# One decoder layer with two kinds of attention: the first stage in another order, the squares from a token-major copy of the input, both rotary tables on VectorE

## The chip, the cores and the metric

The kernel runs on one core of a Trainium2 chip. Its metric is the device time of one execution in microseconds (us). A core has a matrix engine, TensorE (PE in the profile, its weight loads PEld); VectorE (DVE); ScalarE (ACT), which also evaluates functions such as sine and tanh; GpSimd (POOL); and SyncE (SP), which here issues the loads and stores. Each engine has a queue of its own and works through it in order; semaphores hold an instruction until what it reads is there.

## The reference

The reference is one layer for 512 tokens of width 1024 in float32: retention in 8 heads and a sparse attention in 16 query heads and 2 groups side by side, a gated merge, an MLP, and an input of its own for each layer. What matters here is the beginning:

```
def rms_norm(x, g):
    y = x * lax.rsqrt(jnp.mean(x * x, axis=-1, keepdims=True) + 1e-6)
    return y * g

cos_r, sin_r = rope_tables(positions, 128)     # rotary tables of the retention
cos_n, sin_n = rope_tables(positions, 64)      # and of the sparse attention
h = rms_norm(x, norm_mix_g)
proj = h @ w_in                                # queries, keys, values, gates of both
...                                            # sparse attention: kc, vc are compressed to blocks,
                                               # two more keys and two more values are used as they are
x = x + (p @ w_ple_proj) * sigmoid(rms_norm(x, norm_ple_g) @ w_ple_gate)
```

The product `p @ w_ple_proj` needs nothing of the rest, so it can be formed at any time; here it is formed first and parked in memory.

## The kernel before

**Products.** All large products are float32 products made of three products of rounded float32r parts: `mm3` multiplies high by high, high by low and low by high. Each operand has therefore a high part (`hi`, a rounding copy on ScalarE, L206) and a low part (`lo`, the rest, a subtraction on VectorE, L209). Weights come in `Piece`s, mostly 128 x 1024, in three buffers taken in turn (`raw`); a piece is loaded when the third piece ahead of it is used up, and split in halves of 512 columns. `dense` forms 128 x 512 outputs over the eight k-tiles of the normed input, in two items of twelve products, one for each weight half.

**Order.** The program is a list of `Item`s. `run` emits for each item the weight splits that it still needs, its TensorE work, then `look` weight splits ahead (the high parts on ScalarE, the low parts one step behind on VectorE), and last the item's `post`, the work of the other engines on what it left. The order of emission is the order of each engine's queue.

**The first stage** (`start` to `post_nv`). SP loads the per-layer input, its weights, the input transposed (`xT`, 128 x 8 x 512, four loads of 512 KB), the constants, the gains and the positions. TensorE forms the per-layer input product in two halves of four token tiles (`ps_d`, `ps_v`, `ps_s`; copied to `pp_sb` and stored). Beside it ScalarE squares the tiles of `xT` and VectorE adds them into `acc`; sixteen products with a column of ones (L343) sum them over the partitions, `rsqrt` makes the factor of each token, and `over_partitions` spreads the factors over all partitions (`rb`). `make_h` forms the normed tile `ht` from `xT`, gain and `rb` (L511), its high part on ScalarE (L512) and its low part (L514). Eight items with 304 columns (values of the two exact branches and the branch gates, `w_nv`) multiply the normed tiles, tile by tile as they are made; `post_nv` splits the values into `vcat` (L541, L543) and takes the gates' tanh (L542).

**After that** four dense products follow: compressed values (`vc`, `ps_t`), compressed key (`kc`, `ps_t`), two exact keys (`ps_d`, `ps_v`), and then the two compressions and head 0 of the retention. `post_vc` copies the values twice (`dup`, L600, L601) and adds positions (`blk`, L590); `post_kc` turns the key with the table of the sparse attention (`rope_nsa`: VectorE, then a sum `nr` on GpSimd, L532) and copies it twice (L608, L609).

**Rotary tables.** The angles of 512 tokens lie folded as 128 x 256. `reduced` subtracts multiples of two pi, `folded` does so in three steps of falling size (L386), `ends` takes an absolute value and eight sines on ScalarE (L400, L401), which need ScalarE's sine table (ACT_TABLE_LOAD). The table of the sparse attention (`n`) is reduced on GpSimd in the first stage, with its sines between the halves of `vc`; the table of the retention (`r`) is made on VectorE in head 0, its items put in at three places there:

```
items += [vc[0], table_n[1], vc[1], Item(0, lambda: close("nw", "a0"))]
items += [x for x, at in zip(table_r, (0, 4, 5)) if n == at]
```

Of the kernel before, what the change touches and what calls it, by code (L numbers as in the profile page):

```python
# [16 lines left out]
P = 128  # L17
S = 512
# [14 lines left out]
# columns of the constants  # L33
# [3 lines left out]
# columns of the gains  # L37
# [34 lines left out]
def weave(a, b):  # L72
    """Two lists of items merged in proportion to their costs."""
# [13 lines left out]
class Op:  # L87
    """A step of one engine, for arrange(): its time, the steps it needs, the buffers it takes and gives back."""
# [52 lines left out]
def _layer_kernel(ctx, tc, a, out):  # L141
# [4 lines left out]
    # ------------------------------------------------------------------ pools  # L146
# [17 lines left out]
    # the banks of PSUM: two pairs "s", two singles "t", and the singles "v" and "d"  # L164
# [7 lines left out]
    # ------------------------------------------------------- weights, in pieces  # L172
# [15 lines left out]
    def split(n, low=True, eng=dve):  # L188
        """The two parts of the n-th part of a weight, the low one only with low."""
# [23 lines left out]
    def used(p):  # L213
        """The buffer of p has all its readers: the third piece after it may follow."""
# [4 lines left out]
    def defer(fn):  # L219
        """fn is emitted behind the next item on the tensor engine."""  # L220
        deferred.append(fn)

    def run(items):
# [6 lines left out]
        for it in items:  # L230
# [11 lines left out]
            # the low part one step behind the high part, so that neither engine waits for the other  # L242
# [11 lines left out]
    def mm3(ps, sh, sl, mh, ml, first, last):  # L254
        """ps (+)= (sh + sl).T @ (mh + ml), without the product of the two low parts."""
# [4 lines left out]
    def dense(tag, pieces, xs, post, nsub=2, off=0):  # L260
        """ps[n, tok] = sum over the k-tiles of xs(), as nsub items; post(ps) takes it up."""
# [24 lines left out]
    def rsqrt(v, n, tag, eng=dve):  # L286
        """1 / sqrt(v) of a small [128, n] tile: bit estimate, a step of third and one of second order."""
# [24 lines left out]
    def parts(pool_, t, tag, name, late=False, **kw):  # L312
        """hi and lo float32r parts of the SBUF tile t; the low part behind the next item with late."""
# [10 lines left out]
    # -------------------------------------------------------------- constants  # L324
# [11 lines left out]
    def token_rstd(accs, tag):  # L336
        """Items that leave rstd of each token, [128, 4], in T[tag]."""
# [15 lines left out]
    def over_partitions(tag, dst):  # L353
        """An item that puts T[tag] of each token on every partition of dst()."""
# [11 lines left out]
    def table(pool_, name, ci, cs, tmp):  # L366
# [4 lines left out]
        def reduced(pool=dve):  # L371
            ang, kk, kh, t = T[name] = tmp()
            pool.tensor_copy(kk, T["pos_i"])
# [1251 lines left out]
```

## Time and profile before

| | us |
|---|---|
| timed runs, median of 3 (lowest, highest) | 1291.59 (1290.68, 1291.60) |
| profiled execution, span | 1288.7 |
| TensorE busy in it | 1261.2 |
| VectorE busy | 770.6 |
| ScalarE busy | 530.1 |
| GpSimd busy | 230.4 |

The page of the profile gives the profiled execution as its span, from its first to its last instruction; the timed runs also hold what lies around the span, and are 2.0 to 2.9 us longer than it. A row of the timeline is an instruction (or several alike, x2 and more): its start and duration in us, its engine and line, what it writes and reads by the program's names, and in brackets how long the engine had been idle before it and what ended that. A wait is idle time of an engine put down to the instruction that released it. The granted clock of TensorE is a share of 2.4 GHz.

### The profile page before, as it was taken

The page shows a single profiled execution, that of the slowest core. Times are in us where ns is not written, and L with a number is a line of the kernel's source. Part 1 is how long each engine was busy: PE and PEld are TensorE (multiplying, and loading weights), DVE is VectorE, ACT ScalarE, POOL GpSimd, SP SyncE. Part 2 cuts the span into 40 slices and gives each one's busy share as a digit, 9 for nine tenths or more (in the row PEclk, how much of TensorE's full clock was granted, in tenths as well). Part 3 has the DMA queues.
Part 4 walks back from the last instruction along what each step waited for, and adds up shares of the span by engine and source line. Part 5 has one row for each costly group of instructions (what it writes and reads, how often), then busy time and mean ns, then how long its engine had stood idle before and what let it go on. Part 6 is the DMA issues. An engine that isn't in the chain of part 4 may idle for free.

```text
span 1288.7 us, 16807 instructions
## 1 busy us (share of the span) xinstructions
PE 1261.2 (98%) x6312; PEld 1038.0 (81%) x6312; DVE 770.6 (60%) x1398; ACT 530.1 (41%) x1091; POOL 230.4 (18%) x310
## 2 busy tenths in 40 slices
PE   7999999999999999999999999999999999999996
PEld 6867998988988887787888778888888888888885
DVE  7665664557467477678878864556653235544456
ACT  5644333333233233567877652343322223333333
POOL 5230000000000013357664600000000000000035
PEclk9999999999999999999999999999999999999998
DMA  6532223223223232211111022342232343332221
GB/s 244 176 121 88 75 91 98 74 91 98 75 82 105 68 90 82 66 50 33 34 34 34 17 77 90 120 139 83 97 101 95 98 163 99 96 101 94 87 82 66
DMA packets 34673, 116.42 MB, mean 90 GB/s; under 512 B 4128, under 2 KB 4640, under 8 KB 34464
## 3 DMA queue, kind: packets, MB, share of 16 engines
q1 hardware_dynamic: 34592, 115.35, 27.7%
q8 instruction: 50, 0.82, 0.3%
q14 instruction: 31, 0.25, 0.1%
HBM read 111.14 MB, written 4.19 MB: 89 GB/s over the span
## 4 chain that ended last, share of the span: by engine, by line
PE 51%; DVE 1%; POOL 0%; issue 0%; ACT 0%; DVEq 0%
PE ps_s L256 6%; PE ps_s L258 6%; PE ps_s L257 6%; PE ps_d L256 4%; PE ps_d L258 4%; PE ps_d L257 4%; PE ps_v L256 3%; PE ps_v L258 3%; PE ps_v L257 3%; PE ps_t L1085 2%; PE ps_t L257 1%; PE ps_t L258 1%; PE ps_t L256 1%; PE ps_v L1102 1%; PE ps_v L1101 1%; PE ps_s L1009 1%
## 5 line engine op out<-in xcount | busy, mean ns | idle before, releaser
L206 ACT ACTIVATE hi<-raw 128x512 fp32r<-128x512 f32 (+1 forms) x364 | 222.2, 621 | 257.2 <-PE ps_v L258 62.4
L209 DVE TENSOR_TENSOR lo<-raw,hi 128x512 fp32r<-128x512 f32 (+1 forms) x350 | 237.0, 699 | 72.2 <-ACT hi L206 72.1
L209 POOL TENSOR_TENSOR lo_fw<-raw_fw,hi_fw 128x512 fp32r<-128x512 f32 x8 | 11.3, 1435 | 504.2 <-ACT hi_fw L206 504.2
L256 PE MATMUL ps_d<-h_hi,hi 128*128 128x512 f32 x216 | 90.1, 417 | 0.0
L258 PE MATMUL ps_d<-h_hi,lo 128*128 128x512 f32 x216 | 85.4, 395 | 0.0
L257 PE MATMUL ps_d<-h_lo,hi 128*128 128x512 f32 x216 | 85.3, 395 | 0.0
L1062 POOL TENSOR_TENSOR pr<-pr,rr 128x512 f32<-128x512 f32 x80 | 83.7, 1076 | 0.0
L1027 ACT ACTIVATE pr<-ps_s,nm 128x128 f32<-128x128 f32 (+3 forms) x128 | 66.0, 523 | 20.7 <-DVE sc L1021 14.6
L256 PE MATMUL ps_t<-h_hi,hi 128*128 128x512 f32 x168 | 67.4, 401 | 0.0
L302 POOL TENSOR_TENSOR rs_q<-rs_y 128x4 f32<-128x4 f32 (+1 forms) x9 | 4.4, 491 | 351.8 <-DVE rs_y L292 351.8
L257 PE MATMUL ps_t<-h_lo,hi 128*128 128x512 f32 x168 | 66.5, 396 | 0.0
L258 PE MATMUL ps_t<-h_hi,lo 128*128 128x512 f32 x168 | 66.5, 396 | 0.0
L1094 DVE TENSOR_TENSOR ptl<-ps_t,pth 128x512 fp32r<-128x512 f32 x80 | 54.2, 685 | 18.5 <-ACT pth L1089 15.3
L1019 DVE TENSOR_REDUCE nm<-ps_s 128x2 f32<-128x256 f32 (+3 forms) x64 | 52.1, 815 | 15.4 <-PE ps_s L1012 14.7
L1339 ACT ACTIVATE hh<-relu 128x512 fp32r<-128x512 f32 x32 | 20.3, 634 | 93.5 <-DVE relu L1336 93.5
L1089 ACT ACTIVATE pth<-ps_t 128x512 fp32r<-128x512 f32 x80 | 47.3, 597 | 26.4 <-PE ps_t L1085 23.0
L258 PE MATMUL ps_s<-hh,lo 128*128 128x512 f32 x128 | 50.8, 397 | 0.0
L256 PE MATMUL ps_s<-hh,hi 128*128 128x512 f32 x128 | 50.7, 396 | 0.0
L257 PE MATMUL ps_s<-hl,hi 128*128 128x512 f32 x128 | 50.7, 396 | 0.0
L256 PE MATMUL ps_s<-gx_hi,hi 128*128 128x512 f32 x128 | 50.6, 395 | 0.0
L258 PE MATMUL ps_s<-gx_hi,lo 128*128 128x512 f32 x128 | 50.5, 395 | 0.0
L257 PE MATMUL ps_s<-gx_lo,hi 128*128 128x512 f32 x128 | 50.5, 395 | 0.0
(462 smaller groups left out, 3419.2 us busy)
## 6 DMA issues: line engine op xcount, KB each, us to landing
raw<-in_w_ret_qkg_dram SPq DMA_DIRECT2D x32, 512.0 KB, 3.5
raw<-in_w_mlp_up_dram SPq DMA_DIRECT2D x32, 512.0 KB, 3.7
raw<-in_w_mlp_down_dram SPq DMA_DIRECT2D x32, 512.0 KB, 3.7
raw<-in_w_ret_v_dram SPq DMA_DIRECT2D x16, 512.0 KB, 3.5
raw<-in_w_ret_o_dram SPq DMA_DIRECT2D x16, 512.0 KB, 3.5
raw<-in_w_merge_gate_dram SPq DMA_DIRECT2D x16, 512.0 KB, 3.6
raw<-in_w_nsa_dram SPq DMA_DIRECT2D x12, 512.0 KB, 3.5
o_ret<-in_cmp_w_dram SPq DMA_DIRECT2D x8, 512.0 KB, 5.7
```

Of the source, the lines that this page charges most:

```text
L206: act.activation(p.hi[i], p.raw[:, c], AF.Copy)
L209: eng.tensor_tensor(p.lo[i], p.raw[:, c], p.hi[i].bitcast(F32), op=ALU.subtract)
L256: pe.matmul(ps, sh, mh, start=first, stop=False)
L257: pe.matmul(ps, sh, ml, start=False, stop=False)
L258: pe.matmul(ps, sl, mh, start=False, stop=last)
L1019: dve.tensor_reduce(self.nm[:, j, :], self.seen(j), axis=AX.XY, op=ALU.max, negate=True)
L1027: act.activation(self.pr[:, j, br, 0 : self.nk].rearrange("p (b j) -> p b j", j=P), self.seen(j)[:, br], AF.Exp, bias=self.nm[:, j, br : b ...
L1062: pool.tensor_tensor(p, p, self.rr[:, :, 1 + br : 2 + br].broadcast_to([P, 4, P]), op=ALU.mult)
L1085: pe.transpose(self.t[i][:, j * P : (j + 1) * P], self.pr[:, j, br, kb * P : (kb + 1) * P], ident)
L1089: act.activation(hi, self.t[i], AF.Copy)
L1094: dve.tensor_tensor(lo, self.t[i], self.pt[i][0].bitcast(F32), op=ALU.subtract)
L1339: act.activation(hi, t, AF.Square)
```

## The change

- **Start.** Five products on a zeroed tile (`warm`) stand ahead of everything on TensorE. The first piece of the per-layer weights (in two halves), the gains, the positions and the constants are issued on ScalarE's queue instead of SP's.
- **Squares.** The input is given a second time, token-major (`x`, one 128 x 1024 tile for each of the four token tiles, loaded into two buffers `xk`). ScalarE squares each tile and sums its rows in the same instruction (`ss0`). The squares of `xT`, their sums on VectorE and the sixteen products with ones are gone. `first_rstd` makes the factors and halves of them.
- **Value and gate products.** They take `gh`, the parts of input times gain without the factor of the token (`make_g`), so they need not wait for the factors; `post_nv` multiplies the results by each token's factor.
- **Order.** The second half of the per-layer input product stands behind the value and gate products, and all tiles of the normed input but the first half of tile 0 are made behind its four items. The four loads of the compression's first weights are issued later.
- **Rotary tables.** `tables` reduces and folds both in one pass of 512 columns on VectorE: `reduced` behind `vc[0]`, `folded` with the absolute value behind `vc[1]`, the sines of the sparse attention behind `kc[0]`, those of the retention, with a tanh that brings the next function table, behind `kc[1]`. GpSimd has no part in it, and head 0 none.

The diff, cut:

```diff
+        def reduced():
...
+            dve.tensor_copy(kk[:, 0:H], T["pos_i"])
+            for i, ci in enumerate((C_INVN, C_INVR)):
+                dve.tensor_scalar_mul(ang[:, i * H : (i + 1) * H], kk[:, 0:H], cst[:, ci : ci + 1])
+            dve.tensor_scalar(kk, ang, float(1.0 / (2 * np.pi)), MAGIC, op0=ALU.mult, op1=ALU.add)
...
+        def folded():
+            ang, kk, kh = T["tb"]
             for c in (TWO_PI_1, TWO_PI_2, TWO_PI_3):
                 for x in (kh, kk):
...
+                    dve.scalar_tensor_tensor(ang, x, -c, ang, op0=ALU.mult, op1=ALU.add)
+            dve.tensor_scalar(ang, ang, -3.1415925, 3.1415925, op0=ALU.max, op1=ALU.min)
             act.activation(kk, ang, AF.Abs)
+        def ends(n, name, cs):
...
-        return [Item(0, None, f) for f in ((lambda: (reduced(pool), folded(pool)), ends) if name == "n" else (reduced, folded, ends))]
+        return [Item(0, None, f) for f in (reduced, folded, lambda: ends(0, "n", C_SGNN), lambda: ends(1, "r", C_SGNR))]
...
+        for _ in range(5):
+            pe.matmul(ps[:, 0:256], warm[:, 0:128], warm, start=True, stop=True)
...
         for k in range(2):
+            act.dma_start(w0.raw[:, k * S : (k + 1) * S], w0.src[:, k * S : (k + 1) * S])
             sp.dma_start(pT[:, k, :], a["pT"][:, k, :])
...
+        act.dma_start(gains, a["gains"])
         for k in range(0, KT, 2):
             sp.dma_start(xT[:, k : k + 2, :], a["xT"][:, k : k + 2, :])
...
+        act.dma_start(cst, a["consts"])
+        T["xk"] = []
+        for t in range(2):
+            load_token_major(t)
+        issue(w_nv[1])
...
+    def square_x(t):
+        act.activation(T["xk"][t], T["xk"][t], AF.Square, accum_out=T["ss0"][:, t : t + 1])
+        if t + 2 < NQ:
+            load_token_major(t + 2)
+    def first_rstd():
+        v = sm.tile([P, NQ], F32, tag="n0v", name="v")
+        dve.tensor_scalar(v, T["ss0"], 1.0 / D, EPS, op0=ALU.mult, op1=ALU.add)
+        T["n0"] = rsqrt(v, NQ, "n0")
...
+    def make_g(k):
+        hi, lo = T["gh"][k]
+        g = gains[:, G_MIX + k : G_MIX + k + 1]
+        act.activation(hi, T["xT"][:, k, :], AF.Copy, scale=g)
+        dve.scalar_tensor_tensor(lo, T["xT"][:, k, :], g, hi.bitcast(F32), op0=ALU.mult, op1=ALU.subtract)
...
-            act.activation(vcat[:, :, :, t, 0:64], vv, AF.Copy)
+            act.activation(vcat[:, :, :, t, 0:64], vv, AF.Copy, scale=r)
...
-                mm3(T["nv"][t], T["h"][k][0][:, q], T["h"][k][1][:, q], *w, k == 0, k == KT - 1)
+                mm3(T["nv"][t], T["gh"][k][0][:, q], T["gh"][k][1][:, q], *w, k == 0, k == KT - 1)
+        def post(k=k):
+            if k + 5 < KT:
+                make_g(k + 5)
+            if 1 <= k < 5:
+                square_x(k - 1)
+            if k == 4:
+                first_rstd()
+        add(Item(1.5, go, post, w_nv[k // 3].parts(k % 3 * NV, (k % 3 + 1) * NV) if k > 1 else (), 2))
+        if k == 6:
+            add(bc)
+            add(Item(0, None, lambda: make_h(0)))
+    for t in range(NQ):
+        def then(t=t):
+            if t == 0:
+                post_nv()
+            make_h(2 * t + 1)
+            make_h(2 * t + 2)
+        add(pp_item(1, t, w_pp[1].parts() if t == 0 else (), 0 if t < 3 else 2, then))
...
-    items += [vc[0], table_n[1], vc[1], Item(0, lambda: close("nw", "a0"))]
-    items += dense("t", [Piece(a["w_nsa"][0])], hs, post_kc)
+    items += [Item(0, lambda: close("a0")), Item(0, ret_start), Item(0, cmp_start), vc[0], table_items[0], vc[1], table_items[1]]
+    kc = dense("t", [Piece(a["w_nsa"][0])], hs, post_kc)
+    items += [kc[0], table_items[2], kc[1], table_items[3]]
...
-            items += [x for x, at in zip(table_r, (0, 4, 5)) if n == at]
```

Three places in the order of the instructions are spoken of below. A row has the line, the operation, what it writes and reads, and the shape.

VectorE around the factors of the first norm, before: the last steps of `rsqrt` (`rs_y`, `rs_q`, `rs_r`), and behind them the low parts (`lo`) of the value weights for k-tiles 0 and 1 and the first normed tile.

```order
L304 TENSOR_SCALAR rs_r_272<-rs_q_271 128x4
L305 TENSOR_TENSOR rs_r_272<-rs_r_272,rs_q_271 128x4
L300 SCALAR_TENSOR_TENSOR rs_y_270<-rs_r_272,rs_y_270 128x4
L307 TENSOR_TENSOR rs_q_271<-rs_y_270 128x4
L300 SCALAR_TENSOR_TENSOR rs_q_271<-rs_q_271,v_268 128x4
L300 SCALAR_TENSOR_TENSOR rs_y_270<-rs_q_271,rs_y_270 128x4
L209 TENSOR_TENSOR lo_294<-raw_158,hi_292 128x304
L209 TENSOR_TENSOR lo_298<-raw_158,hi_296 128x304
L511 SCALAR_TENSOR_TENSOR ht_323<-xT_124,gains_73,rb_163 128x512
```

And now: behind the factors stand their halves (`n0h`) and the low weight parts for k-tiles 6 and 7.

```order
L300 SCALAR_TENSOR_TENSOR rs_y_350<-rs_r_352,rs_y_350 128x4
L307 TENSOR_TENSOR rs_q_351<-rs_y_350 128x4
L300 SCALAR_TENSOR_TENSOR rs_q_351<-rs_q_351,v_348 128x4
L300 SCALAR_TENSOR_TENSOR rs_y_350<-rs_q_351,rs_y_350 128x4
L488 TENSOR_SCALAR n0h_362<-rs_y_350 128x4
L209 TENSOR_TENSOR lo_376<-raw_170,hi_345 128x304
L209 TENSOR_TENSOR lo_392<-raw_170,hi_378 128x304
L528 SCALAR_TENSOR_TENSOR ht_404<-xT_129,gains_73,rb_172 128x512
L209 TENSOR_TENSOR lo_419<-raw_268,hi_396 128x512
```

The two low weight parts that stood behind the factors before were those of the first k-tiles; they have gone ahead of them, and those of the last two stand there.

The same engine from there on to the low weight part of `vc`'s first half, before (`lo_500`); the rows of `vcat` are the value splits.

```order
L514 TENSOR_TENSOR h_lo6_109<-ht_427,h_hi6_108 128x512
L209 TENSOR_TENSOR lo_465<-raw_237,hi_447 128x304
L514 TENSOR_TENSOR h_lo7_111<-ht_449,h_hi7_110 128x512
L209 TENSOR_TENSOR lo_482<-raw_237,hi_467 128x304
L209 TENSOR_TENSOR lo_500<-raw_367,hi_486 128x512
L543 TENSOR_TENSOR vcat_91<-ps_d_347,vcat_91 128x4x64
L543 TENSOR_TENSOR vcat_91<-ps_v_348,vcat_91 128x4x64
L543 TENSOR_TENSOR vcat_91<-ps_s_349,vcat_91 128x4x64
L543 TENSOR_TENSOR vcat_91<-ps_s_350,vcat_91 128x4x64
L544 TENSOR_SCALAR gate_78<-gate_78 128x192
L209 TENSOR_TENSOR lo_547<-raw_367,hi_502 128x512
L209 TENSOR_TENSOR lo_553<-raw_445,hi_551 128x512
```

And now: that low part is `lo_503`, and the normed tiles stand ahead of it. The rows left out are the next four of the same kind.

```order
L528 SCALAR_TENSOR_TENSOR ht_450<-xT_129,gains_73,rb_172 128x512
L531 TENSOR_TENSOR h_lo0_97<-ht_404,h_hi0_96 128x512
...
L528 SCALAR_TENSOR_TENSOR ht_472<-xT_129,gains_73,rb_172 128x512
L531 TENSOR_TENSOR h_lo3_103<-ht_468,h_hi3_102 128x512
L528 SCALAR_TENSOR_TENSOR ht_486<-xT_129,gains_73,rb_172 128x512
L531 TENSOR_TENSOR h_lo4_105<-ht_472,h_hi4_104 128x512
L528 SCALAR_TENSOR_TENSOR ht_490<-xT_129,gains_73,rb_172 128x512
L531 TENSOR_TENSOR h_lo5_107<-ht_486,h_hi5_106 128x512
L209 TENSOR_TENSOR lo_503<-raw_343,hi_501 128x512
```

The normed tiles have moved from ahead of the value splits to between these and the weight of `vc`.

ScalarE ahead of the weight of the second exact key, before: the copies of the compressed values (`dup1`), of the compressed key (`dup0`), and the high parts of the weights, `hi_655` being the one for the second half of the second exact key.

```order
L601 ACTIVATE dup1_521<-ps_t_534 64x511
L206 ACTIVATE hi_610<-raw_484 128x512
L206 ACTIVATE hi_628<-raw_549 128x512
L608 ACTIVATE dup0_520<-nr1_630 64x512
L609 ACTIVATE dup0_520<-nr1_630 64x511
L608 ACTIVATE dup0_520<-nr1_630 64x512
L609 ACTIVATE dup0_520<-nr1_630 64x511
L206 ACTIVATE hi_655<-raw_549 128x512
L206 ACTIVATE hi_673<-raw_580 128x512
L621 ACTIVATE kc1_0_87<-nr1_675 64x4x128
```

And now, where the same part is `hi_687`; the rows left out are four more sines.

```order
L645 ACTIVATE dup0_531<-nr1_652 64x511
L401 ACTIVATE sin_r_527<-tb_564,cst_72 64x256
L402 ACTIVATE cos_r_526<-tb_564,half_pi_77 64x256
...
L401 ACTIVATE sin_r_527<-tb_564,cst_72 64x256
L402 ACTIVATE cos_r_526<-tb_564,half_pi_77 64x256
L405 ACT_TABLE_LOAD
L405 ACTIVATE tanh_670<-half_pi_77 128x1
L206 ACTIVATE hi_687<-raw_556 128x512
L206 ACTIVATE hi_705<-raw_588 128x512
```

The eight sines of the retention's table, a table load and a tanh stand now between the copies of the compressed key and that weight part.

## Rows read from the trace of the kernel before

**Rows 1.** The page, part 1: busy time of each engine.
```profile
PE 1261.2 (98%) x6312; PEld 1038.0 (81%) x6312; DVE 770.6 (60%) x1398; ACT 530.1 (41%) x1091; POOL 230.4 (18%) x310
```

**Rows 2.** Waits of TensorE, 0 to 150 us: total, times, longest.
```profile
PE ps_d L256 <- ACT hi L206: 5.9, 1, 5.9
PE ps_v L258 <- DVE lo L209: 2.1, 1, 2.1
PE ps_d L257 <- DVE lo L209: 1.3, 3, 0.5
```

**Rows 3.** Timeline of TensorE: start, duration, operation, [idle before it and releaser].
```profile
14.31 0.35 PE L343 MATMUL ps_t<-ones,acc 128*128 128x2 f32 x2 [0.62 <-DVE acc L471]
16.09 0.48 PE L256 MATMUL ps_d<-hi,ph 128*128 128x512 f32 x1
...
28.87 0.41 PE L258 MATMUL ps_d<-hi,h_lo 128*128 128x304 f32 x1 [0.53 <-DVE h_lo L514]
...
39.18 0.30 PE L256 MATMUL ps_d<-hi,h_hi 128*128 128x304 f32 x1
...
40.86 0.39 PE L256 MATMUL ps_t<-h_hi,hi 128*128 128x512 f32 x1
...
60.65 0.40 PE L256 MATMUL ps_v<-h_hi,hi 128*128 128x512 f32 x1
...
86.70 0.39 PE L256 MATMUL ps_d<-hi,h_hi 128*128 128x256 f32 x1
```

**Rows 4.** By stretches: length, busy PE, PEld, DVE, ACT, POOL, granted clock, DMA share, GB/s.
```profile
10.00:20.00 10.00, 9.38 (x43) 7.51 (x42) 8.40 (x20) 4.94 (x10) 6.51 (x8) 0.83 0.95 323
...
80.00:90.00 10.00, 8.98 (x42) 6.62 (x43) 5.28 (x12) 3.00 (x7) 0.00 (x0) 0.83 0.75 263
```

**Rows 5.** Timeline of SP: the load of the positions.
```profile
5.85 1.81 SPq L410 DMA_DIRECT2D pos_i<-in_positions_dram  x2
```

**Rows 6.** Timeline of ScalarE, five of its rows.
```profile
42.90 1.28 ACT L400 ACT_TABLE_LOAD   x1
44.20 0.51 ACT L400 ACTIVATE sin_n<-tb,cst 64x256 f32<-64x256 f32 x1
...
47.88 0.64 ACT L206 ACTIVATE hi<-raw 128x512 fp32r<-128x512 f32 x1
48.42 0.57 ACT L600 ACTIVATE dup<-ps_t 64x512 f32<-64x512 f32 x1
...
59.37 1.15 ACT L206 ACTIVATE hi<-raw 128x512 fp32r<-128x512 f32 x2
```

**Rows 7.** DMA issues, 0 to 60 us: count, KB each, median us to landing.
```profile
xT<-in_xT_dram SPq DMA_DIRECT2D x4, 512.0 KB, 6.3
...
raw<-in_w_nsa_dram SPq DMA_DIRECT2D x4, 512.0 KB, 3.8
```

**Rows 8.** Timeline of VectorE, eight of its rows.
```profile
16.27 0.16 DVE L348 TENSOR_SCALAR v<-ps_t 128x4 f32<-128x4 f32 x1
...
18.39 0.16 DVE L300 SCALAR_TENSOR_TENSOR rs_y<-rs_q,rs_y 128x4 f32<-128x4 f32 x1
...
24.33 1.22 DVE L511 SCALAR_TENSOR_TENSOR ht<-xT,gains,rb 128x512 f32<-128x512 f32 x1
...
35.72 0.74 DVE L511 SCALAR_TENSOR_TENSOR ht<-xT,gains,rb 128x512 f32<-128x512 f32 x1
36.38 0.68 DVE L514 TENSOR_TENSOR h_lo<-ht,h_hi 128x512 fp32r<-128x512 f32 x1
...
40.31 0.42 DVE L543 TENSOR_TENSOR vcat<-ps_d,vcat 128x256 fp32r<-128x256 f32 x1 [1.28 <-ACT gate L542]
...
49.63 2.34 DVE L590 TENSOR_TENSOR blk<-dup,pes 128x248 f32<-128x248 f32 x4 [5.66 <-ACT dup L601]
...
91.40 2.70 DVE L386 SCALAR_TENSOR_TENSOR tb<-tb 128x256 f32<-128x256 f32 x6
```

**Rows 9.** Timeline of GpSimd: the sum behind the compressed key.
```profile
55.15 1.61 POOL L532 TENSOR_TENSOR nr<-nr,nr 128x512 f32<-128x512 f32 x1 [19.42 <-DVE nr L529]
```

More of the change, by code (lines that the diff above doesn't have):

```diff
@@ L399, in ends @@
                     c_ = slice(H * i, H * i + H)
[L400 to L401 removed]
+                    act.activation(T["sin_" + name][r_, c_], ang[x_, s_], AF.Sin, scale=cst[x_, cs + o : cs + o + 1])
+                    act.activation(T["cos_" + name][r_, c_], kk[x_, s_], AF.Sin, bias=half_pi[x_], scale=-1.0)
             if name == "r":
                 act.activation(sm.tile([P, 1], F32, tag="tanh", name="tanh"), half_pi, AF.Tanh)
[L406 removed]
+        return [Item(0, None, f) for f in (reduced, folded, lambda: ends(0, "n", C_SGNN), lambda: ends(1, "r", C_SGNR))]
     def load_positions(t):
         for i in range(2):
[L410 to L417 removed]
+            act.dma_start(t[64 * i : 64 * i + 64], a["positions"][:, i * (S // 2) : (i + 1) * (S // 2)].broadcast_to([64, S // 2]))
+    table_items = tables()
     w_pp = [Piece(a["w_ple_proj"][i]) for i in range(2)]
@@ L458, in start @@
             split_part(w_pp[0], k)
-        T["acc"] = ap.tile([P, S], F32, name="acc")
         T["rb"] = ap.tile([P, S], F32, name="rb")
-        for k in range(4):
-            square_x(k)
-        T["acc_b"] = ap.tile([P, S], F32, name="acc_b")
-        pool.tensor_tensor(T["acc_b"], xT[:, KT - 2, :], xT[:, KT - 2, :], op=ALU.mult)
-    def square_x(k):
-        sq = T["acc"] if k == 0 else P_["a0"].tile([P, S], F32, tag="sq", name="sq", bufs=2)
-        act.activation(sq, T["xT"][:, k, :], AF.Square)
-        if k:
-            dve.tensor_tensor(T["acc"], T["acc"], sq, op=ALU.add)
@@ new lines, in start, with load_token_major @@
+        T["gh"] = [(ap.tile([P, S], F32R, name=f"gh_hi{k}"), ap.tile([P, S], F32R, name=f"gh_lo{k}")) for k in range(KT)]
+        T["ss0"] = sm.tile([P, NQ], F32, tag="ss0", name="ss0")
+        make_g(0)
+    def load_token_major(t):
+        T["xk"].append(P_["a0"].tile([P, D], F32, tag="xk", name="xk", bufs=2))
+        sp.dma_start(T["xk"][t], a["x"][:, t, :])
+    def square_x(t):
+        act.activation(T["xk"][t], T["xk"][t], AF.Square, accum_out=T["ss0"][:, t : t + 1])
+        if t + 2 < NQ:
+            load_token_major(t + 2)
@@ new lines, in _layer_kernel, with pp_item, go, post @@
+    add(Item(0, start))
+    def pp_item(nh, t, parts_=(), look=0, then=None):
+        def go():
+            w = w_pp[nh]
+            T["pp"] = bank("dvss"[t] if nh == 0 else "ttdv"[t])
+            q = slice(t * P, (t + 1) * P)
+            for k in range(2):
+                mm3(T["pp"], T["p"][k][0][:, q], T["p"][k][1][:, q], *w.cols(k * S, (k + 1) * S), k == 0, k == 1)
+        def post():
+            sb = P_["a0"].tile([P, S], F32, tag="pps", name="pp_sb", bufs=4)
+            if nh == 0 and t % 2:
+                dve.tensor_scalar_mul(sb, T["pp"], 0.5)
+            else:
+                act.activation(sb, T["pp"], AF.Copy, scale=0.5)
+            sp.dma_start(pp_dram[:, t, nh * S : (nh + 1) * S], sb)
+            if then:
+                then()
+        return Item(1.3, go, post, parts_, look)
@@ L507, in make_h @@
+    for t in range(NQ):
+        early = {0: w_pp[0].parts(), 2: [(w_nv[0], 0)], 3: [(w_nv[0], 1)]}
+        add(pp_item(0, t, early.get(t, ()), 0, lambda t=t: make_g(t + 1)))
     def make_h(k):
@@ L514, in make_h @@
             dve.tensor_tensor(T["h"][k - 1][1], T["ht", k - 1], T["h"][k - 1][0].bitcast(F32), op=ALU.subtract)
-    add(Item(0, None, lambda: make_h(1)))
     hs = (lambda: T["h"], KT)
@@ L554, in go @@
                 q = slice(t * P, (t + 1) * P)
-                mm3(T["nv"][t], T["h"][k][0][:, q], T["h"][k][1][:, q], *w, k == 0, k == KT - 1)
-        add(Item(1.5, go, post_nv if k == KT - 1 else None, w_nv[k // 3].parts(k % 3 * NV, (k % 3 + 1) * NV) if k > 1 else (), 2))
+                mm3(T["nv"][t], T["gh"][k][0][:, q], T["gh"][k][1][:, q], *w, k == 0, k == KT - 1)
[10 more added lines that the diff above has]
+            add(Item(0, None, lambda: make_h(0)))
+    for t in range(NQ):
+        def then(t=t):
[4 more added lines that the diff above has]
+        add(pp_item(1, t, w_pp[1].parts() if t == 0 else (), 0 if t < 3 else 2, then))
     def cmp_start():
@@ L567, in cmp_start @@
         sp.dma_start(T["mask"], a["mask"])
-        for c in range(4):
-            load_cmp(1, c)
         for x in T["dup"]:
             pool.memset(x[64:128, :, S - 1 : S], 0.0)
-    add(Item(0, None, cmp_start))
+    add(Item(0, None, lambda: [load_cmp(1, c) for c in range(4)]))
     w_cmp = [[Piece(a["cmp_w1"][i, c], width=0, keep="oret") for c in range(4)] for i in range(2)]
```

106 lines of the change are left out of this document (32 added, 74 removed).

## The prediction

> **What bounds the kernel now.** I read the summary of busy time first, then the waits of TensorE in the first 150 us, then busy time by stretches, then the matmuls in order of time, and last VectorE and ScalarE beside them. TensorE is busy 98% of the span [rows 1], so all of its work is on the path and a change can take away or add only stalls, slow clock and products of its own. The stalls lie at the start: 5.9 us until the first weight half is there, 1.3 us for low weight parts and 0.5 for one low tile in the value and gate products, 2.1 us in the first head [rows 2], and 0.6 ahead of the tiny products of the sums of squares, the row at 14.31 [rows 3]. Two ten-microsecond stretches show a granted clock of 0.83 [rows 4]: of 2.4 GHz and 1.2 GHz, the two levels, 3.4 us went at the lower, so each stretch lost 1.7 us; TensorE had waited or run tiny products just before [rows 2, 3]. From the first product of head 0's values, at 86.70 us [rows 3], both programs issue the same steps. So I follow the new queues to that product; the difference there is the difference at the end.
>
> Durations come from one profiled execution with a span of 1288.7 us; the timed runs lie 2.0 to 2.9 us above it, which I take as the same for both kernels, and I add the difference to the median, 1291.59.
>
> **What goes.** The sixteen tiny products with their wait: 14.31 to 16.09 us plus 0.6 [rows 3], 2.4 us, and the slow stretch behind them, 1.7. The waits of the value and gate products, 1.8. The wait of 2.1 us in the first head, because the second table no longer runs on VectorE there, and the slow stretch behind it, 1.7. Together 9.7 us. GpSimd's table work and VectorE's six sums go too, but they were under the products.
>
> **What comes, in the order of the path.**
>
> *The start* is not on the new path unless it gets 4 us worse. ScalarE now issues six loads (the two of positions took 1.81 us on SP [rows 5]; the four others I put at 0.45 each, half a position load) and only then loads its table, 1.28 [rows 6], so its first activation begins at about 6.0 us, and the first real product at 7.2 instead of 5.9. The five warm-up products cost nothing, as nothing is there to multiply. If they keep the clock high, the first half of the input product ends near 13.9, about as before.
>
> *The squares.* Ahead of the first token-major square ScalarE's queue holds 17 activations: 11 of 512 columns at 0.54 (47.88 to 48.42 [rows 6]), two evictions at 0.6 (the copy out of PSUM at 48.42 took 0.57 [rows 6]), four splits of 304 columns, put at 0.4; 8.7 us, and about 2.0 of waits for products: it starts at 16.7. A square of 1024 columns does not occur before; I take 1.1, twice 0.54 (bounds 0.6 and 1.3). Two buffers hold token tiles, so the third load is issued when the first square ends, 17.8, and the fourth after the second, 19.8. A 512 KB load took 3.8 to 6.3 us to land [rows 7]; with 5.0 the third lands at 22.8, the fourth at 24.8, and the last square ends at 25.9. The factors take 2.3 (16.27 to 18.39 and 0.2 [rows 8]) and one scaling: 28.5. On VectorE the split for k-tile 6 stands behind them, 0.5 more. TensorE could start k-tile 6 at 24.6 (six k-tiles of 1.68, 39.18 to 40.86 [rows 3], behind 13.9, with 0.6 of waiting). It starts at 29.0: 4.4 us idle (2.0 with loads of 3.8, 7.0 with 6.3).
>
> *The normed tiles.* K-tiles 6 and 7 take 3.4, the spreading of the factors (four float32 products of 128 columns, 0.2 each, estimate) 0.8, the first product group of the second half 1.4, and three waits for weight splits 1.0: 6.6, to 35.6; with one slow stretch as in [rows 4], 37.3. Now VectorE and ScalarE turn to what used to lie under the products: eviction 0.6, the four value splits of 0.42 [rows 8] behind ScalarE's copies with the gate, 2.5, and then twelve operations on the normed tiles, of 0.63 each (from 35.72 to 36.38, where one follows another, it is 0.66 [rows 8]), 7.6; the high part of tile 6 and then of the next weight on ScalarE, 0.6. That is 11.4: the compressed-value product starts at 48.7. TensorE has three product groups of 1.4 to do in that time, so it idles about 6.8 us. Its low weight part comes 0.6 later; 24 products take 5.6 (84 of them from 40.86 to 60.65, 0.235 each [rows 3]); for the clock, which I expect to have dropped, 2.0, a little over a slow stretch [rows 4]: the end is at 56.8. Before, it was at 40.86 plus 5.6, 46.5.
>
> *The tables.* Behind that product stands one chain: four copies of 0.6 (48.42 [rows 6]) 2.6; two of the block sums (2.34 for four [rows 8]) 1.2; six folds and a clip. Of 256 columns the folds took 2.70, 0.45 each [rows 8]; of 512 I take 0.64 for each of the seven, 4.5 in all (bounds 3.15, at no growth, and 6.3, at twice), as the operation of 512 columns at 35.72 does [rows 8]. Then on ScalarE the absolute value 0.65, one weight split 0.53, table load 1.28, eight sines 3.68 (44.20 to 47.88 [rows 6]); on VectorE two rotary products 1.3; the sum on GpSimd 1.6 [rows 9] and 0.1; four copies 2.6; eight more sines 3.7, the table load 1.3, one tanh 0.1; and only then, with 0.6, the high part of the second half of the second key's weight. Sum 25.7. Before, that split followed the four copies directly, ending at 59.37 plus 0.6 [rows 6], and TensorE began that half without a wait at 60.65 [rows 3]. Now it begins at 82.5. The waits ahead of the first key (about 3 us) and of the first half of the second (2 us) lie inside this chain and cost nothing more.
>
> The Trainium skill (ScalarE: Activation LUTs, What ACT_TABLE_LOAD costs) has a table switch at 2.66 us, 1.28 of load and 1.38 of drain. The rows show no drain: the load begins at 42.90 and the first sine at 44.20 [rows 6]. By the page the chain, with two switches in it, would be 2.8 us longer and the time 1314; the trace decides.
>
> *The rest.* Before, from 60.65 to 86.70 it is 26.05, of which 2.1 wait and 1.7 slow clock go: 22.2. After so long a stall I add 2.0 for the clock again. 82.5 + 22.2 + 2.0 = 106.7, against 86.70: 20.0 us more. The weight loads for all this are issued while TensorE idles and hide there.
>
> **Forecast.** 1291.6 + 20.0 = 1311.6, slower by 1.5%.
>
> **Rivals.**
> 1. *Faster.* The 9.7 us go and nothing takes their place: 1281.9. For it: GpSimd leaves VectorE alone, and the gain of a tile then costs 0.74 instead of 1.22 (24.33 and 35.72 [rows 8]). Against it: twelve operations stand between the value splits and the next weight, and three product groups give 4.2 us; it would need 0.35 us for each, half of what the rows show. That is the point from which it decides. 8%.
> 2. *Milder stalls.* All waits come, but the clock holds (5.7 less) and token tiles land in 3.8 us (2.4 less): 1291.6 + 11.9 = 1303.5. For it: the wait of 0.53 us at 28.87 us [rows 3] lies in no slow stretch. Against it: the wait of 2.1 us in the first head [rows 2] does [rows 4]. 23%.
> 3. *The table chain is hidden*, because ScalarE reaches the key's weight earlier than its order says: only the first two stalls count, 56.8 less 46.5 is 10.3, and 3.8 come back in the first head: 1298.1. Against it: the split stands behind the sines in one queue. 10%, of which 4 within what can be told from no change.
> 4. *Longer.* Loads of 6.3 us (2.6 more) and one or two more slow stretches: 1316 to 1318, because the second copy of the input adds 2 MB where the loads were already busiest. 10%.
>
> **How the numbers follow.** The forecast has 49%, with its own range 1307 to 1316. From 1300 to 1318 it takes in rival 2, most of 4 and the upper part of 3, and leaves out about 18%. Faster or slower by 0.2%, 2.6 us, is about what a measurement of this kernel can tell from no change: faster 8%, within 4%, slower 88%.
>
> **What would show it.** In the new profile TensorE should wait about 4 us for a weight split behind the factors near 25 us, about 7 us ahead of the first product of the compressed values near 42, and for 6 to 9 us in the second key, released by ScalarE's split, with sixteen sines in front of it. Head 0's value products should start near 107 us. The forecast is wrong if ScalarE or VectorE gets to those splits before TensorE does, if the fourth token tile lands before 20 us, or if steps behind head 0 change.

## The result, and the profile after

The changed kernel takes 1308.11 us, the median of 4 runs (1306.51 to 1309.76), against 1291.59 before: 16.5 us more. The ratio on record is 1.0135 with an interval of 1.0123 to 1.0147; the quotient of these two medians is 1.0128 and lies inside it. The forecast was 1311.6. The profiled execution has a span of 1307.9 us, 19.2 more than the one before; it belongs to the slowest of the four runs, and that before, by its span, to the fastest (1290.68), so the spans lie 2.7 us further apart than the medians.

TensorE is busy 1266.1 us, almost as long as before [rows 1], in a longer span. Its waits by the releasing instruction in the first 170 us (total, times, longest) are no longer those of [rows 2]:

```profile
PE ps_t L256 <- ACT hi L206: 6.9, 1, 6.9
PE ps_v L256 <- ACT hi L206: 6.8, 1, 6.8
PE ps_d L257 <- DVE lo L209: 5.0, 1, 5.0
PE ps_d L258 <- DVE lo L209: 3.0, 1, 3.0
PE ps_d L256 <- ACT hi L206: 1.8, 1, 1.8
```

On TensorE's timeline (start, duration, operation, idle before it and releaser) the first two rows are the first product of the per-layer input and the first of the value products. The next four are the stalls in order of time: k-tile 6 of the value products, the compressed values, the first exact key and the second half of the second one. The last row is head 0's first value product:

```profile
7.50 0.79 PE L256 MATMUL ps_d<-hi,ph 128*128 128x512 f32 x1 [1.77 <-ACT hi L206]
...
16.20 0.30 PE L256 MATMUL ps_d<-hi,gh_hi 128*128 128x304 f32 x1
...
32.12 0.62 PE L257 MATMUL ps_d<-lo,gh_hi 128*128 128x304 f32 x1 [4.96 <-DVE lo L209]
...
52.88 0.79 PE L256 MATMUL ps_t<-h_hi,hi 128*128 128x512 f32 x1 [6.93 <-ACT hi L206]
...
70.16 0.50 PE L258 MATMUL ps_d<-h_hi,lo 128*128 128x512 f32 x1 [3.01 <-DVE lo L209]
...
87.06 0.80 PE L256 MATMUL ps_v<-h_hi,hi 128*128 128x512 f32 x1 [6.81 <-ACT hi L206]
...
111.65 0.39 PE L256 MATMUL ps_d<-hi,h_hi 128*128 128x256 f32 x1
```

What each waited for stands in the queues of the two other engines. VectorE sat idle 6.5 us until the last square, then made the factors, and only then the low weight part for k-tile 6. Later the block sums waited for their positions, and the six folds (`tb`) stood behind the sums, ahead of the low weight part of the first exact key:

```profile
29.52 0.17 DVE L485 TENSOR_SCALAR v<-ss 128x4 f32<-128x4 f32 x1 [6.50 <-ACT xk L479]
...
31.59 0.86 DVE L209 TENSOR_TENSOR lo<-raw,hi 128x304 fp32r<-128x304 f32 x2
...
62.76 2.06 DVE L626 TENSOR_TENSOR blk<-dup,pes 128x248 f32<-128x248 f32 x4 [1.92 <-DMA pes<-in_cmp_pe_dram]
64.74 4.30 DVE L389 SCALAR_TENSOR_TENSOR tb<-tb 128x512 f32<-128x512 f32 x6
```

ScalarE waited for the third and fourth token-major tile (2.52 and 1.81 us). Its split for the compressed values, at 52.21, stands behind the normed tiles (`h_hi`), and that for the second key, at 86.39, behind the copies of the compressed key, eight sines, a table load and a tanh:

```profile
25.04 1.06 ACT L479 ACTIVATE xk<-xk 128x1024 f32<-128x1024 f32 x1 [2.52 <-DMA xk<-in_x_dram]
...
28.34 1.06 ACT L479 ACTIVATE xk<-xk 128x1024 f32<-128x1024 f32 x1 [1.81 <-DMA xk<-in_x_dram]
...
51.67 0.63 ACT L529 ACTIVATE h_hi<-ht 128x512 fp32r<-128x512 f32 x1 [0.63 <-DVE ht L528]
52.21 1.13 ACT L206 ACTIVATE hi<-raw 128x512 fp32r<-128x512 f32 x2
...
70.71 1.28 ACT L401 ACT_TABLE_LOAD   x1
72.00 0.51 ACT L401 ACTIVATE sin_n<-tb,cst 64x256 f32<-64x256 f32 x1
...
84.50 0.49 ACT L402 ACTIVATE cos_r<-tb,half_pi 64x256 f32<-64x256 f32 x1
84.99 1.28 ACT L405 ACT_TABLE_LOAD   x1
86.28 0.20 ACT L405 ACTIVATE tanh<-half_pi 128x1 f32<-128x1 f32 x1
86.39 1.13 ACT L206 ACTIVATE hi<-raw 128x512 fp32r<-128x512 f32 x2
```

Around the three long stalls the granted clock is low, as in [rows 4] (it is 0.83 from 70 to 80 us too, behind the wait of 3.0); the columns are those of that group:

```profile
30.00:40.00 10.00, 7.88 (x35) 7.24 (x35) 3.90 (x14) 2.11 (x4) 0.00 (x0) 0.66 0.18 52
...
50.00:60.00 10.00, 7.12 (x21) 5.61 (x22) 9.09 (x18) 5.34 (x10) 0.00 (x0) 0.66 0.61 197
...
80.00:90.00 10.00, 3.19 (x9) 2.32 (x8) 2.96 (x6) 7.42 (x15) 0.28 (x1) 0.77 0.11 22
```

One thing does not fit. Head 0's values begin 24.95 us later than before [rows 3], yet the end comes only 19.2 later. The same two products in the two timelines, the scores of head 0 and a transpose in the last stage, first before:

```profile
127.25 0.42 PE L256 MATMUL ps_t<-rqh,rkh 128*128 128x384 f32 x1 [0.91 <-DVE kc L699]
...
1228.32 0.60 PE L1400 MATMUL ps_t<-cst,x 128*128 128x128 f32 x4
```

and then after:

```profile
152.21 0.41 PE L256 MATMUL ps_t<-rqh,rkh 128*128 128x384 f32 x1 [0.90 <-DVE kc L742]
...
1247.57 0.60 PE L1433 MATMUL ps_t<-cst,x 128*128 128x128 f32 x4
```

The lag of 24.96 us has shrunk to 19.25. Matched product by product, it stays at 24.8 to 24.95 until 750 us and then falls in two kinds of stretch only: the products on `nph` and `npl` (attention output) and on `gx_hi` and `gx_lo` (MLP input). There TensorE issues 512-column products closer together, with no wait on either side. Twelve products in a row, half of one output tile, before:

```profile
876.32 0.40 PE L256 MATMUL ps_v<-gx_hi,hi 128*128 128x512 f32 x1
...
878.88 0.40 PE L258 MATMUL ps_v<-gx_hi,lo 128*128 128x512 f32 x1
```

and after:

```profile
900.05 0.39 PE L256 MATMUL ps_v<-gx_hi,hi 128*128 128x512 f32 x1
...
902.55 0.39 PE L258 MATMUL ps_v<-gx_hi,lo 128*128 128x512 f32 x1
```

From the first start to the last it is eleven spacings: 2.56 us before (0.233 each) and 2.50 after (0.227). Some 960 such products give 5.6 us.

### The profile page after: what moved, and what is told of

Its sections match the earlier page's. It is cut to its first block, busy times and chain, and to the rows that moved or that the text cites. A ratio compares the mean times of both kernels' runs of the same rounds, so it can differ in the third digit from the quotient of the medians.

```text
span 1307.9 us, 16793 instructions
## 1 busy us (share of the span) xinstructions
PE 1266.1 (97%) x6306; PEld 1046.2 (80%) x6306; DVE 766.8 (59%) x1402; ACT 533.0 (41%) x1097; POOL 210.1 (16%) x290
## 4 chain that ended last, share of the span: by engine, by line
PE 50%; DVE 1%; POOL 0%; issue 0%; ACT 0%; DVEq 0%
PE ps_s L256 6%; PE ps_s L257 6%; PE ps_s L258 6%; PE ps_d L256 4%; PE ps_d L257 4%; PE ps_d L258 4%; PE ps_v L256 3%; PE ps_v L257 3%; PE ps_v L258 3%; PE ps_t L1118 2%; PE ps_t L257 1%; PE ps_t L258 1%; PE ps_t L256 1%; PE ps_v L1135 1%; PE ps_v L1134 1%; PE ps_s L1042 1%
## 5 line engine op out<-in xcount | busy, mean ns | idle before, releaser
L258 PEld LDWEIGHTS ps_d<-h_hi,lo 128*128 128x128 f32 x216 | 41.0, 190 | 13.2 <-DVE lo L209 3.5
```

The source lines that it names most:

```text
L258: pe.matmul(ps, sl, mh, start=False, stop=last)
```

## The experiments

Ratios are against the kernel before on the same chip; the changed kernel has 1.0135 (1.0123 to 1.0147). Where two kernels are compared "by the ratios", it is the difference of their ratios, times the 1291 us of the kernel before.

**Where the 5.6 us come from.** The change adds two small tiles, `ss0` and `n0h`, to the pool of small tiles, which grows by 128 bytes; all tiles allocated after it on that side move by as much. In the built programs `gx_hi0` starts at 66944 before and at 67072 after (128 and 0 modulo 256), while the normed tiles `h` stay at 224, `hh` at 160 modulo 256. The theory of place says that this is what counts, its rival that the history of the execution does. Unused tiles (pads) and other pools move the tiles:

```diff
# b_padl: the kernel before
+    sm.tile([P, 16], F32, tag="pad", name="pad")
# a_nopad: the changed kernel
-        T["ss0"] = sm.tile([P, NQ], F32, tag="ss0", name="ss0")
+        T["ss0"] = ap.tile([P, NQ], F32, name="ss0")
...
-        T["n0h"] = sm.tile([P, NQ], F32, tag="n0h", name="n0h")
+        T["n0h"] = P_["a0"].tile([P, NQ], F32, name="n0h")
# b_padr: the kernel before
+        hp.tile([P, 56], F32, name="pad_h")
...
+        fp.tile([P, 40], F32, name="pad_f")
```

> The kernel before with one more unused tile of 64 bytes, twice, in the pool of small tiles, so that every tile that comes after it on that side lies 128 bytes further, among them the tiles of the attention's output (nph, npl) and of the MLP's input (gx_hi, gx_lo), which then start at a multiple of 256 bytes as they do in the changed kernel. Theory place: the 958 products on them come 0.0058 us closer to each other, as in the changed kernel, so 1291.6 - 5.6 = 1286.0. Rival history: these products ran faster in the changed kernel because of what came before them (clock, phase of the transfers), so nothing changes: 1291.6.

> The changed kernel with its two new small tiles (ss0, n0h) in the pool of the first stage instead of the pool of small tiles, so that gx and nph lie where they lay before; the instructions and their order are the same. Theory place: the 5.6 us that came back after 750 us are lost, 1308.1 + 5.6 = 1313.7. Rival history: no change, 1308.1.

> The kernel before with 224 unused bytes behind the normed tiles and 160 behind the tiles of the last stage, so that the tiles on the other side (normed tiles h, rth, rtl, m, hh, hl) start at multiples of 256 bytes, and gx and nph stay where they were. Theory place, if the start modulo 256 is what counts: some 2670 products of 512 columns on these tiles go from 0.2335 to 0.227 us each, 17 us less, 1274. If it is the start modulo 512 (these tiles come to lie at 256 of 512, gx in the changed kernel at 0 of 512): no change, 1291.6. Rival history: no change, 1291.6.

Measured: the displaced kernel before 1285.34 (0.9955, 0.9938 to 0.9971), 4.7 us less than before on that chip; the changed kernel without the displacement 1314.14 (1.0186, 1.0171 to 1.0201), 6.0 more than the changed kernel (6.6 by the ratios); the other side displaced 1278.40 (0.9906, 0.9891 to 0.9921), 11.7 less. The history is ruled out: unused bytes alone move the time, and the changed kernel loses its gain when only the two tiles move. The third run came 5 us short of its 17: the products on `h` gained 0.005 us each and not 0.0065, some 2 us for 1340 of them, and the rest of the gap is not settled. Groups of products by shape (count, busy, mean ns of one) of that run: `gx`, left in place, has the long products and `hh` the short ones:

```profile
L256 PE MATMUL ps_s<-gx_hi,hi 128*128 128x512 f32 x128 | 50.6, 395 | 0.0
...
L256 PE MATMUL ps_s<-hh,hi 128*128 128x512 f32 x128 | 49.8, 389 | 0.0
```

and of the changed kernel, where it is the other way round:

```profile
L256 PE MATMUL ps_s<-hh,hi 128*128 128x512 f32 x128 | 50.8, 397 | 0.0
...
L256 PE MATMUL ps_s<-gx_hi,hi 128*128 128x512 f32 x128 | 49.9, 390 | 0.0
```

Both displacements together (`b_padlr`), and other offsets (`b_offs`: pads of 64, 160 and 128 bytes in the same three places):

> The kernel before with both displacements, of the attention's output and the MLP's input and of the tiles on the other side. Theory place: the two add up, 4.7 and 11.7 less than before, 1290.1 - 16.4 = 1273.7. Rival: what counts is how far the tile streamed and the tile of weights lie from each other, so the two partly cancel: 1278 or more.

> The kernel before with other displacements: gx and nph start at 192 modulo 256 bytes, h, rth, rtl and m at 64, hh and hl at 32. If only multiples of 256 help: spacings of 0.232 to 0.235 us in all of them, and about 1291. If multiples of 64 are enough: gx, h, rth, m at 0.226 to 0.229, hh at 0.234, and about 1278.

Measured: 1271.84 (0.9850, 0.9835 to 0.9864), 19.4 less than before on that chip: they add up, with 3 us on top of the 16.4 of the two alone, which lies within the intervals. The other offsets: 1281.7 in a single run. Neither answer was right: at 64 modulo 256 the products on `h`, `rth` and `m` were nearly as close as at 0, at 192 (`gx`) and 32 (`hh`) as wide as before.

**The wait for k-tile 6.**

```diff
# a_xk4: the changed kernel; the tile of the warm-up products lies elsewhere to make room
-tag="xk", name="xk", bufs=2)
+tag="xk", name="xk", bufs=4)
...
+        for t in range(2, NQ):
+            load_token_major(t)
...
-            if k == 4:
+            if k == 5:
                 first_rstd()
```

> The changed kernel with four buffers for the token-major tiles, so that no load waits for a square, and the factors of the first norm made one item later, behind the low weight parts that stood behind them (the tile of the warm-up products lies elsewhere to make room). Theory queue: the wait of 5 us for k-tile 6 is the low weight part behind the factors, and these behind the last load, which waits for a buffer; it goes, with the slow stretch behind it (0.66 from 30 to 40 us, 3.4 us): 1301 to 1304. Rival bandwidth: the transfers are at their limit till 23 us, the tiles land no earlier and the wait only moves to the spreading of the factors: 1307 to 1309.

Measured: 1301.02 (1.0078, 1.0063 to 1.0093), 7.4 us less than the changed kernel by the ratios. The four squares follow each other from 18.9 to 24.8 us, none waits for a load, and the wait is gone; the other three stand as they were. So it was the buffers and the place of the factors in VectorE's queue (changed together here), not the transfers' rate. The waits of this run:

```profile
PE ps_v L256 <- ACT hi L206: 7.7, 2, 6.8
PE ps_t L256 <- ACT hi L206: 6.9, 1, 6.9
PE ps_d L258 <- DVE lo L209: 2.9, 1, 2.9
```

**The wait for the compressed values.**

```diff
# a_vclook: the changed kernel
-        add(pp_item(1, t, w_pp[1].parts() if t == 0 else (), 0 if t < 3 else 2, then))
+        add(pp_item(1, t, w_pp[1].parts() if t == 0 else (), 2, then))
```

> The changed kernel with the weight splits for the compressed values ahead of the normed tiles 1 to 8 on ScalarE and VectorE. Theory queue: the wait of 6.9 us goes, the product begins near 46 us and takes the tiles as they come, one every 1.3 us, so it ends at 55 to 56 instead of 61; behind it the block sums wait for their positions, which land at 62.7 behind the stores of the per-layer product on SP, so only 1 to 3 us are left at the end: 1305 to 1307. Rival: the weights were never what came last, the tiles were; the product begins no earlier than 51 and the time is 1308.

Measured: 1307.58 (1.0129, 1.0112 to 1.0146), not to be told from the changed kernel, and above the 1305 to 1307 expected. The wait of 6.9 went, and the product took the normed tiles one by one; but then its second half waited for its own low weight part, which still stands behind the tiles, and the block sums waited 2.4 us for their positions:

```profile
46.06 0.50 PE L257 MATMUL ps_t<-h_lo,hi 128*128 128x512 f32 x1 [0.31 <-DVE h_lo L531]
47.32 0.50 PE L257 MATMUL ps_t<-h_lo,hi 128*128 128x512 f32 x1 [0.30 <-DVE h_lo L531]
...
53.77 0.72 PE L258 MATMUL ps_t<-h_hi,lo 128*128 128x512 f32 x1 [3.43 <-DVE lo L209]
```

**The tables' chain.** The sines of the second table later, and the angles earlier:

```diff
# a_sinr: the changed kernel
-    items += [kc[0], table_items[2], kc[1], table_items[3]]
+    items += [kc[0], table_items[2], kc[1]]
...
     items += dense("v", [Piece(a["w_nsa"][3])], hs, post_key(1))
+    items.append(table_items[3])
# a_early: the changed kernel; the angles lie in a pool of their own, open till the heads end
             if k == 4:
+                table_items[0].post()
+                table_items[1].post()
                 first_rstd()
```

> The changed kernel with the eight sines of the retention's table (and the tanh behind them) put behind the second exact key instead of behind the compressed key. Theory queue: the wait of 6.8 us ahead of the second half of the second key is ScalarE's queue, and 5.0 us of it are these sines; it shrinks to 1.8, and a part comes back as the sines now stand ahead of weight splits of head 0: 1303 to 1306. Rival: that half waits for something that came as late (weights, VectorE's low part), so the wait stays and the time is 1308.

> The changed kernel with the angles of both tables reduced and folded ahead of the factors of the first norm on VectorE, where it waited 6.5 us for the squares, instead of behind the compressed values. Theory queue: the wait of 3.0 us in the first exact key goes, the 6.8 in the second shrink by about 2, the one for k-tile 6 grows by about 2, since 8.3 us of work stand where 6.5 were idle: 1304 to 1306. Rival: the folds are not in the chain (the sines wait for the sine table or for the key's product), and only the 2 us for k-tile 6 are seen: 1310.

Measured: `a_sinr` 1306.85 (1.0130, 1.0115 to 1.0145), in time not to be told from the changed kernel and short of the gain expected. The wait in the second key shrank to 1.8 as forecast, and 4.4 us came back in front of the last part of head 0's output gate, where the sines stand now:

```profile
78.75 0.50 PE L256 MATMUL ps_v<-h_hi,hi 128*128 128x512 f32 x1 [1.77 <-ACT hi L206]
...
100.90 0.80 PE L256 MATMUL ps_v<-h_hi,hi 128*128 128x512 f32 x1 [4.44 <-ACT hi L206]
```

`a_early` 1304.25 (1.0101, 1.0086 to 1.0116), 4.4 less by the ratios. The wait of 3.0 is gone, that in the second key is 6.0, that for k-tile 6 is 7.4: the folds were in the chain, and what covers them in the first stage is too short by 2.4 us.

```profile
PE ps_d L257 <- DVE lo L209: 7.7, 2, 7.4
PE ps_t L256 <- ACT hi L206: 6.9, 1, 6.9
PE ps_v L256 <- ACT hi L206: 6.0, 1, 6.0
```

**Parts alone.** The kernel before with the new `tables` in the new places, and the changed kernel without the warm-up products:

```diff
# b_tables: the kernel before, with tables() of the changed one
-    add(table_n[0])
...
+    items += [Item(0, lambda: close("a0")), Item(0, ret_start), vc[0], table_items[0], vc[1], table_items[1]]
+    kc = dense("t", [Piece(a["w_nsa"][0])], hs, post_kc)
+    items += [kc[0], table_items[2], kc[1], table_items[3]]
...
-            items += [x for x, at in zip(table_r, (0, 4, 5)) if n == at]
# a_nowarm: the changed kernel
-        for _ in range(5):
-            pe.matmul(ps[:, 0:256], warm[:, 0:128], warm, start=True, stop=True)
```

> The kernel before with the table part of the change alone: both tables on VectorE together behind the halves of the compressed values, the sines behind the halves of the compressed key (the positions are still loaded by SP), the rest as before. Theory queue: the chain from the end of the compressed values (46.5 us) to the weight of the second key's second half takes the 25.9 us that it took in the changed kernel, so that half starts at 72.4 instead of 60.65, 11.7 later; 3.8 come back in head 0 and about 2 go to the clock: 1291.2 + 9.9 = 1301. Rival: the chain hurts only because the first stage ends late, with VectorE and ScalarE behind; alone it is mostly covered: 1291 to 1295.

> The changed kernel without the five warm-up products. Theory: they keep nothing warm, since they end 1.8 us before the first real product and the products behind them ran at the lower clock till 13.6 us all the same: no change, 1307.5 to 1308.7. Rival: they do raise the clock earlier, by up to 2 us: 1310.

Measured: `b_tables` 1298.23 (1.0057, 1.0042 to 1.0072), 7.3 us more than before. The waits of the keys are there, 2.85 and 6.81 us for 3.01 and 6.81, although the first stage is the old one. The first row is the start of the compressed values:

```profile
36.99 0.39 PE L256 MATMUL ps_t<-h_hi,hi 128*128 128x512 f32 x1
...
51.66 0.50 PE L258 MATMUL ps_d<-h_hi,lo 128*128 128x512 f32 x1 [2.85 <-DVE lo L209]
...
68.55 0.80 PE L256 MATMUL ps_v<-h_hi,hi 128*128 128x512 f32 x1 [6.81 <-ACT hi L206]
```

So the chain does not hang on a late first stage. My sum was 2.6 too high, because the table part also gives something in the first stage, which I had not counted: the compressed values begin at 36.99 instead of 40.86 [rows 3]. With GpSimd's table work gone VectorE's gain of a tile takes 0.75 us instead of 1.02 and the waits of the value products go: from the first of these to the compressed values it is 14.0 us instead of 16.6. Of the 3.9 us that is 2.6; the rest is mainly the slow stretch of [rows 4], 10 to 20 us, which this execution does not have (granted clock 1.00). That cannot be put down to GpSimd, since `b_padr`, where GpSimd does the table, has none there either. The rows of the two gains (count, busy, mean ns), in `b_tables`:

```profile
L505 DVE SCALAR_TENSOR_TENSOR ht<-xT,gains,rb 128x512 f32<-128x512 f32 x8 | 5.9, 748 | 1.1 <-ACT rb L361 1.1
```

and before:

```profile
L511 DVE SCALAR_TENSOR_TENSOR ht<-xT,gains,rb 128x512 f32<-128x512 f32 x8 | 8.0, 1015 | 1.3 <-ACT rb L361 1.3
```

So the change splits, by the ratios, into 0.0057 for the table part (7.4 us), 0.0129 for the first stage (16.7; `a_nopad`, all of it but the place, less `b_tables`), and 0.0051 given back by the place (6.6), 0.0135 together. The first stage was not run alone, so its share holds whatever the two parts cost each other. `a_nowarm` 1308.23 (1.0132, 1.0117 to 1.0147): the warm-up products are worth nothing here.

**A version that beats both.** `b_padlr` with the retention's table spread over the keys:

```diff
# b_best: b_padlr
-    items += dense("d", [Piece(a["w_nsa"][2])], hs, post_key(0))
-    items += dense("v", [Piece(a["w_nsa"][3])], hs, post_key(1))
+    items += [k0[0], table_r[0], k0[1], k1[0], table_r[1], k1[1]]
...
-            items += [x for x, at in zip(table_r, (0, 4, 5)) if n == at]
+            items += [x for x, at in zip(table_r[2:], (0, 5)) if n == at]
```

> The kernel before with both displacements, and the retention's table spread over the keys: reduced behind the first half of the first exact key, folded in two parts behind the first half of the second one and in head 0, the sines where they were. Theory: the wait of 2.5 us in head 0 and the slow stretch behind it (0.83 from 80 to 90 us, 1.7 us) go and nothing else waits: 1271.8 - 4.2 = 1267.6. Rival: the pieces delay low weight parts of the keys, and the wait only moves there: 1271 to 1272.

Measured: 1268.96 (0.9831, 0.9815 to 0.9847), the fastest of all, 1.7% under the kernel before. Against `b_padlr` (0.9835 to 0.9864) the intervals overlap. The wait of 2.5 us that `b_padlr` has in head 0 is gone and the granted clock is 1.00 there (0.83 from 80 to 90 us in `b_padlr`). In its place 1.1 us has come up earlier in head 0, in its output gate behind a low weight part, and 0.2 in the first exact key: the rival's mechanism, at another place and for a part.

```profile
69.71 0.50 PE L259 MATMUL ps_d<-h_hi,lo 128*128 128x512 f32 x1 [1.14 <-DVE lo L210]
```

## Why the prediction was right, and where it was not

| mark, us | before | forecast | after |
|---|---|---|---|
| first half of the per-layer product ends | 13.7 | 13.9 | 16.4 |
| idle ahead of k-tile 6 | | 4.4 | 5.0 |
| TensorE goes on with k-tile 6 | | 29.0 | 32.12 |
| compressed values begin | 40.86 | 48.7 | 52.88 |
| second half of the second key begins | 60.65 | 82.5 | 87.06 |
| head 0's values begin | 86.70 | 106.7 | 111.65 |
| end of the span | 1288.7 | +20.0 | +19.2 |

- **The three stalls are right, in place, releaser and size**: 5.0 for 4.4, 6.9 for 6.8, 6.8 in the second key for "6 to 9". `a_xk4` took the first away. `a_vclook` took the second, and 3.4 us of it came back as a wait for the low part. `a_sinr` cut the third to 1.8. The 6.8 is not what its own terms give: 11.4 less three groups of 1.4 is 7.2.
- **The chain of 25.7** from the end of the compressed values to the split took 25.9 (61.1 to 87.0). Its first terms were other than I had them: all four block sums stand ahead of the folds and wait for their positions, 3.6 us from 61.1 to 64.74 where I had copies and two sums, 3.8. That these agree is luck. The second table load came without a drain too: the load begins at 84.99 and the tanh at 86.28. By an estimate from the page of the Trainium skill (ScalarE: Activation LUTs, What ACT_TABLE_LOAD costs), 1.38 of drain at each of two switches, the chain would have been 2.8 longer; the trace decides, and it has none.
- **The start was mis-sized by 2.5.** I wrote "If they keep the clock high, the first half of the input product ends near 13.9". They did not: from 8.89 to 13.6 the products follow each other at 0.43 us, as in the slow stretch of [rows 4], and from then on at 0.23. (The granted clock reads 1.00 for the whole time; that it is the lower level is inferred from the spacing.) In `a_sinr`, with the same warm-up, the first products that do not wait go at 0.23 and those from 9.85 to 13.2 at 0.43, with a granted clock of 0.84 from 10 to 20 us. In `a_nowarm`, without it, the spacing of 0.43 ends at 10.9, and the time is the same.
- **The squares were mis-timed, and the fourth load mis-sized.** The first square began at 19.04 and not at 16.7, because ScalarE waited 3.7 us for products at the slow start where I had 2.0. So the third load, which took 4.8 us of the 5.0 that I gave it, was issued 2.4 later; the fourth took 6.1. The factors began 3.6 later than worked out, and k-tile 6 went on 3.1 later. TensorE came late to it as well, so only 0.6 of this is idle time. My bounds for the stall, 2.0 and 7.0, counted the two loads one behind the other; the fourth is issued at the end of the second square whatever the third does, so 3.8 or 6.3 us a load give 3.2 or 5.7.
- **The step that failed** is "the difference there is the difference at the end". The instructions behind head 0 are the same, as I said, but not their time: 5.6 us came back in products whose tiles lie elsewhere. I had compared the order of the instructions and not the addresses. That the forecast of 20 came as close as it did is luck: a path that was 5 us longer than worked out (4.2 of it by the compressed values) and a gain of 5.6 that I did not see nearly cancel.
- **Rival 1** (faster) falls: head 0's values begin 25 us later. Its argument that GpSimd leaves VectorE alone is right, and is worth 2.6 us in `b_tables`.

## What to carry to other kernels

Work that is moved into a queue counts with everything that is queued behind it: here sines and folds, a few microseconds each, stood in front of the weight splits that TensorE needed next, and a wait taken away at one place came back where the same work was put (`a_sinr`, `a_vclook`). A change in the size of one early tile moves all later ones, so compare the spacing of products far from the change before a gain or loss is put down to the change itself.

## What the runs showed of the hardware that was not expected

The distance from one 512-column product to the next depends on where its two input tiles start. One of them is streamed (128x512), the other is held as the weights (128x128, loaded by PEld). Mean spacings of consecutive products, worked out from the timelines of TensorE (those between 0.20 and 0.26 us apart, without a wait), by the start of the streamed tile modulo 256 bytes; the held tiles of these products, the weight parts, start at multiples of 256 in all these programs:

| streamed tile | start: spacing, us |
|---|---|
| `gx_hi`, `gx_lo` | 128: 0.233 (before); 0: 0.227 (after, `b_padl`); 192: 0.233 (`b_offs`) |
| `hh`, `hl` | 160: 0.234 (before, after); 0: 0.227 (`b_padr`); 32: 0.233 (`b_offs`) |
| `h_hi`, `h_lo` | 224: 0.233 (before, after); 0: 0.228 (`b_padr`); 64: 0.230 (`b_offs`) |
| `rth`, `rtl` | 224: 0.233 (before); 0: 0.227 (`b_padr`); 64: 0.229 (`b_offs`) |

Starts at a multiple of 256 were the best in every tile of this table, and a start at 64 nearly as good. The held tile counts as well. In the last stage the parts of the gate weights (`hi_fw`, `lo_fw`) are streamed and `gx` is held. Their spacing is 0.233 before (160 streamed, 128 held), 0.234 in `b_padl` (160, 0), 0.233 in `b_padr` (0, 128), and 0.227 only in `b_padlr` (0, 0). One group of these products (count, busy, mean ns), in `b_padr`:

```profile
L256 PE MATMUL ps_t<-hi_fw,gx_hi 128*128 128x512 f32 x16 | 6.3, 395 | 0.0
```

and in `b_padlr`:

```profile
L257 PE MATMUL ps_t<-hi_fw,gx_hi 128*128 128x512 f32 x16 | 6.2, 389 | 0.0
```

Nor is it enough that both lie alike. The 512-column scores of the retention have both tiles (`rqh`, `rkh`) at 224 before and go at 0.233; with both at 0 (`b_padr`) they go at 0.227. Why stays open. For a kernel that is 98% TensorE it was worth 1.5% (`b_padlr`).
